# A ring of four work tiles with slots of 4352 bytes, and one head's softmax division moved up 450 places in a planner's list

## The chip, the cores and the metric

The kernel runs on one core of a Trainium2 chip. Its time is the device time of one execution in microseconds (us). Two kernels are compared by the medians of several executions each. The profile is of one execution and gives each engine's instructions: PE is the matrix engine, PEld its weight loads, DVE the vector engine, ACT the scalar engine, POOL the GpSimd engine, and SP the queue that issues most of the DMAs.

## The reference

The program is one layer of a decoder trunk over 1040 positions (16 meta tokens and 1024 tokens) and 1024 channels, in float32:

```python
h = rms_norm(h_res, pre_norm_g[i])
z = h @ w_in[i]                       # 1024 x 7328
y_a = (pool_mixer(...)      * silu(pg)) @ w_out_pool[i]
y_b = (mla_attention(...)   * silu(mg)) @ w_out_mla[i]     # 8 heads
y_c = (conformer_conv(...)  * silu(cg)) @ w_out_conf[i]
y_d = (short_conv(...)      * silu(sg)) @ w_out_sc[i]
m = gts[0] * y_a + gts[1] * y_b + gts[2] * y_c + gts[3] * y_d
h_res = h_res + rms_norm(m @ w_o[i], post_norm_g[i])
```

In the attention a head's scores are masked causally, put through a softmax and multiplied with the values. The division by the softmax's sum is done last, on the head's 64 x 1024 output: that is the "division" of this document.

## The kernel before, in words

Each float32 operand of a matrix product is split in a high and a low part, and a product is made as three products of the parts (`split`, line 498: ACT copies the high part, POOL or DVE subtracts it to get the low part). The two big projections use a Strassen scheme, so their operands are sums of blocks. Work goes in three stages.

**Stage one** (to line 1405) makes `z` by the input projection. PE goes through the blocks of `w_in`; beside it, four lanes of small tasks run (lines 1353 to 1363): convolutions, the attention's queries, keys and values, norms, the splitting of weights. Their tiles come from rings of slots. One of them is the ring `t4` (line 566), four slots in pool `tp`, which hold tiles of up to 4160 bytes a partition: parts of `x`, `cq`, `qn`, `ckv`, `khl`, `vhl` and others, and `kone` (line 983), a row of -1.0 that goes to DRAM once.

**Stage two** (lines 1410 to 1702) is the attention, in 16 steps of one head `h` and one half `c` of the queries. Between the products of a head, `refill` (line 1644) puts in the output projections of the three other branches (`fills`, line 1603). One such unit is six products into a bank `ps_y`, of which there are two, an evacuation `th <- (th + 1) * ps_y` on DVE and an addition `m <- m + th`, most of them on DVE. The next but one unit can begin only when the evacuation has emptied its bank.

For heads 0 to 6 the division is done by `sums` (line 1558) and `head_out` (line 1584): a DMA takes the row of sums out of `ol` into `lc`, DVE takes its reciprocal, a DMA writes it to DRAM (`r`), a DMA reads it back broadcast over 64 partitions (`rb`), and DVE multiplies the halves of `ol` with it into `op[c]`. For the last head PE itself spreads the reciprocals (`sums_pe`, line 1569). Heads come in pairs: after the second head of a pair, POOL multiplies `op[c]` with the gate (`smg`), and `split` makes `boM[c][h // 2]` of it, ACT the high part and POOL the low part. Each of `rb`, `op[0]` and `op[1]` has one slot.

**Stage three** (from line 1707) is the attention's own output projection into `ps_u`, which needs all `boM`, and then the last projection `w_o` with the final norm.

**What sets the order.** Nothing is issued when it is recorded. `Plan.record` gives each operation a number `prio = len(self.ops) - self.lift` (line 336), and `plan.ahead(n)` adds n to `lift` for what is recorded inside it: a positive n moves an operation up, a negative one down. `Plan.flush` (line 364) then plays the recorded stage through with rough costs of its own and, whenever an engine is free, gives it the ready operation of the smallest number whose slots are free (line 418). The order that comes out is what each engine runs, in that order and without overtaking. A DMA counts in it as landed 4500 ns after its transfer (line 448), and in `sums` 5000 ns more for those into SBUF (line 1562). Each stage ends with a `flush`, so no operation of a stage can go behind one of the next. Fills are recorded with -400 (line 1648), the division of heads 0 to 6 with -450, and the last head's with 300 (line 1691).

**Where the tiles lie.** `Pool.lay_out` (line 186) rounds a slot up to the pool's grain, 64 bytes for `tp` and `up`, and 256 bytes for the large pools, whose start it also moves to 64 bytes past a multiple of 256 (`PLACE`). Pools of stages two and three begin again where `const` ends, so their places do not depend on `tp`.

## Time and profile before

| | |
|---|---|
| median of 3 runs | 969.21 us (969.03 to 969.52) |
| the profiled execution | 968.91 us |
| its span, first to last instruction | 967.1 us |
| busy: PE, DVE, POOL, ACT | 950.4, 696.0, 678.0, 449.1 us |
| mean granted clock of PE | 0.997 |

A row of the timeline has the start, the duration, the engine, the line, the operation, what is written and read, and the shape; `x2` are two instructions in one row, and square brackets hold the time that the engine was idle before it, with what ended it. All instructions are recorded through one helper and so have line 362; they are told apart by their tiles.

### The profile page before, as it was taken

What the parts mean: (1) busy time and instruction counts of PE and PEld (TensorE: products, weight loads), DVE (VectorE), ACT (ScalarE), POOL (GpSimd) and SP (SyncE); (2) the same over time, 40 slices, a digit from 0 to 9 for tenths busy, and PEclk for the clock granted to TensorE, in tenths of its full rate; (3) what the DMA queues carried; (4) which work ended last, traced back from release to release, by engine and by line L of the source; (5) the groups of instructions that cost most, each with busy time, mean ns of one, the idle gap of its engine ahead of it and who ended that gap; (6) DMA issues with size and microseconds to landing.
All of it is one profiled execution on the core that took longest, in us unless ns stands there. A gap on an engine that the chain in (4) does not pass through costs nothing.

```text
span 967.1 us, 15247 instructions
## 1 busy us (share of the span) xinstructions
PE 950.4 (98%) x5003; PEld 808.9 (84%) x5003; DVE 696.0 (72%) x1113; ACT 449.1 (46%) x914; POOL 678.0 (70%) x628
## 2 busy tenths in 40 slices
PE   8999999999999999999999999999999999999996
PEld 7999899889888887888888878888888788788885
DVE  5856959988779855544536768346778889799757
ACT  7743233444344455554444344366555555225622
POOL 5957555666576787896679679655567786647955
PEclk9999999999999999999999999999999999999998
DMA  8145566668787687787655688699899664783633
GB/s 258 45 126 144 167 198 213 216 196 270 231 265 255 205 248 214 220 255 216 195 168 169 205 268 276 208 318 262 272 221 297 175 187 132 272 267 95 211 113 142
DMA packets 136330, 203.03 MB, mean 210 GB/s; under 512 B 19672, under 2 KB 83159, under 8 KB 135483
## 3 DMA queue, kind: packets, MB, share of 16 engines
q1 hardware_dynamic: 127274, 185.28, 63.3%
q10 hardware_dynamic: 8656, 15.74, 4.4%
q0 software_dynamic: 320, 1.05, 0.3%
q8 instruction: 39, 0.64, 0.3%
q14 instruction: 41, 0.33, 0.1%
HBM read 129.11 MB, written 72.88 MB: 209 GB/s over the span
## 4 chain that ended last, share of the span: by engine, by line
PE 90%; POOL 3%; DVE 2%; issue 2%; ACT 1%; DMA 1%; DVEq 0%; SPq 0%; POOLq 0%; ACTq 0%
PE ps_pa L362 16%; PE ps_pb L362 16%; PE ps_pc L362 15%; PE ps_o L362 9%; PE ps_y L362 8%; PE ps_s L362 8%; PE ps_pd L362 7%; PE ps_u L362 7%; PE ps_x L362 5%; POOL S L362 1%; POOL lsq L362 1%; ACT junk L362 1%; DVE c L362 0%; DMA lacc<-acc 0%; POOL u L362 0%
## 5 line engine op out<-in xcount | busy, mean ns | idle before, releaser
L362 PE MATMUL ps_pb<-T,S 128*128 128x512 f32 (+2 forms) x792 | 172.0, 359 | 0.0
L362 PE MATMUL ps_pa<-B,A 128*128 128x512 f32 (+2 forms) x792 | 171.7, 360 | 0.0
L362 POOL TENSOR_TENSOR A<-raw,A 128x512 fp32r<-128x512 f32 x84 | 114.3, 1368 | 61.3 <-ACT A L362 47.7
L362 PEld LDWEIGHTS ps_pb<-T,S 128*128 128x128 f32 x792 | 134.3, 189 | 22.4 <-issue 1.2
L362 PEld LDWEIGHTS ps_pa<-B,A 128*128 128x128 f32 x792 | 134.4, 188 | 22.3 <-issue 1.0
L362 POOL TENSOR_TENSOR S<-ss,S 128x512 fp32r<-128x512 f32 x84 | 116.0, 1393 | 51.8 <-ACT S L362 51.7
L362 POOL TENSOR_TENSOR pt<-p,pt 128x512 fp32r<-128x512 f32 (+1 forms) x96 | 102.8, 1094 | 52.5 <-PE ps_s L362 32.6
L362 DVE TENSOR_TENSOR u<-ps_pb,u 128x512 f32<-128x512 f32 (+2 forms) x66 | 40.3, 610 | 87.4 <-PE ps_pb L362 84.3
L362 DVE SCALAR_TENSOR_TENSOR ps_w<-conv,par,ps_w 128x512 f32<-128x512 f32 x116 | 87.1, 751 | 2.3
L362 PE MATMUL ps_y<-bo,whl 128*128 128x512 f32 x288 | 85.7, 403 | 0.9 <-DVE th L362 0.9
L362 PE MATMUL ps_pc<-B,S 128*128 128x512 f32 (+1 forms) x396 | 85.8, 358 | 0.0
L362 ACT ACTIVATE S<-ss 128x512 fp32r<-128x512 f32 x84 | 50.4, 627 | 74.5 <-DVE ss L362 43.7
L362 PE MATMUL ps_pd<-T,A 128*128 128x512 f32 (+2 forms) x396 | 84.9, 359 | 0.0
L362 PE MATMUL ps_pc<-T,S 128*128 128x512 f32 (+1 forms) x396 | 84.4, 359 | 0.0
L362 ACT ACTIVATE p<-ps_s 128x512 f32<-128x512 f32 (+4 forms) x112 | 49.7, 444 | 60.3 <-PE ps_s L362 29.2
L362 PEld LDWEIGHTS ps_pc<-T,S 128*128 128x128 f32 x396 | 66.8, 188 | 11.2 <-issue 0.7
L362 PEld LDWEIGHTS ps_pd<-T,A 128*128 128x128 f32 x396 | 67.1, 189 | 10.7
L362 PEld LDWEIGHTS ps_pc<-B,S 128*128 128x128 f32 x396 | 66.4, 189 | 10.2
L362 PE MATMUL ps_o<-pt,vt 128*128 128x512 f32 (+7 forms) x288 | 68.7, 346 | 0.2 <-ACT ol L362 0.2
L362 PE MATMUL ps_s<-qt,kt 100*128 100x512 f32 (+4 forms) x336 | 67.8, 324 | 0.0
L362 PEld LDWEIGHTS ps_s<-qt,kt 100*128 100x128 f32 (+1 forms) x336 | 54.1, 176 | 10.3 <-DVE qt L362 0.6
L362 ACT ACTIVATE A<-raw 128x512 fp32r<-128x512 f32 x84 | 52.0, 626 | 22.3 <-PE ps_pd L362 9.7
(281 smaller groups left out, 1890.4 us busy)
## 6 DMA issues: line engine op xcount, KB each, us to landing
raw<-in_w_in_dram SPq DMA_DIRECT2D x52, 512.0 KB
th<-th SPq DMA_DIRECT2D x32, 512.0 KB
th<-z ACTq DMA_DIRECT2D x60, 256.0 KB
v<-vhl SPq DMA_DIRECT2D x16, 384.0 KB
qt<-q SPq DMA_DIRECT2D x16, 384.0 KB
vt<-v SPq DMA_DIRECT2D x8, 768.0 KB
bo<-bo SPq DMA_DIRECT2D x6, 1024.0 KB
w_out_mla<-whl SPq DMA_DIRECT2D x16, 256.0 KB
```

The source lines that it names most:

```text
L362: getattr(self.handle[o["eng"]], o["op"])(*map(real, o["args"]), **{k: real(v) for k, v in o["kw"].items()})
```

## The change

The tile `kone` is made with 1088 columns, of which the first 1040 are used as before, so the largest tile of the ring `t4` has 4352 bytes and each of its four slots gets as many. The division of head 6, the seventh of the eight, is recorded with 0 and not with -450: its three DMAs (`lc`, `r`, `rb`), its reciprocal and its two multiplications stand 450 places further up in the list. Nothing is computed otherwise, and no instruction is added or taken away.

```diff
@@ -980,7 +980,7 @@
-        t = t4([4, L], name="kone")
+        t = t4([4, LK], name="kone")[:, :L]
         POOL.memset(t, -1.0)
         ld(ones_dram, t)
@@ -1688,7 +1688,7 @@
-        with plan.ahead(300 if h == H - 1 else -450):
+        with plan.ahead(300 if h == H - 1 else 0 if h == H - 2 else -450):
             if h == H - 1:
                 head_out(h, c, sums_pe(h, c))
             elif c:
```

`L` is 1040 and `LK` is 1088 (lines 35 and 50); the block of line 1691 does something only for `c == 1` where `h` is 0 to 6.

## The prediction, made before the changed kernel was built

> **What bounds the kernel now.** I read the page's busy times first, then the busy times by stage, then PE's waits, then the timeline where a wait falls behind the change.

> ```profile
> PE 950.4 (98%) x5003; PEld 808.9 (84%) x5003; DVE 696.0 (72%) x1113; ACT 449.1 (46%) x914; POOL 678.0 (70%) x628
> ```
> ```profile
> 25.00:300.00 275.00, 274.37 (x1750) 249.62 (x1750) 220.82 (x347) 114.99 (x243) 179.72 (x167) 1.00 0.61 190
> 300.00:640.00 340.00, 339.22 (x1510) 277.81 (x1509) 198.95 (x262) 152.15 (x277) 261.58 (x235) 1.00 0.73 223
> ...
> 826.00:838.00 12.00, 11.09 (x54) 8.40 (x53) 11.54 (x18) 1.86 (x3) 6.45 (x6) 1.00 0.67 242
> 838.00:958.00 120.00, 119.96 (x541) 99.55 (x539) 98.05 (x118) 47.96 (x96) 81.26 (x59) 1.00 0.53 178
> 958.00:967.00 9.00, 0.00 (x0) 0.00 (x0) 5.45 (x12) 0.90 (x4) 3.79 (x4) 0.64 0.47 176
> ```
> ```profile
> PE ps_s L362 <- ACT p L362: 1.0, 1, 1.0
> PE ps_y L362 <- DVE th L362: 0.9, 1, 0.9
> ```

> PE's column follows the length of each stretch: 274.4 of 275, 339.2 of 340, 120.0 of 120. So PE is the bound, at a clock of 1.00, and time goes only where PE idles: 0.9 us in 826 to 838, and the last 9 us, which have no product at all. Of PE's waits the second row is the one in reach of the change: the unit of fills that waits for an evacuation `th`. That bounds what the change can give directly.

> ```profile
> 833.16 2.34 PE L362 MATMUL ps_y<-bo,whl 128*128 128x512 f32 x9
> 836.41 1.67 PE L362 MATMUL ps_y<-bo,whl 128*128 128x512 f32 x6 [0.91 <-DVE th L362]
> ```
> ```profile
> 825.41 0.69 DVE L362 SCALAR_TENSOR_TENSOR th<-th,ps_y 128x512 f32<-128x512 f32 x1 [3.58 <-PE ps_y L362]
> 826.13 0.84 DVE L362 TENSOR_TENSOR m<-m,th 128x512 f32<-128x512 f32 x1
> 827.00 0.68 DVE L362 TENSOR_TENSOR op<-ol,ps_s 64x512 f32<-64x512 f32 x1
> 827.72 0.69 DVE L362 SCALAR_TENSOR_TENSOR th<-th,ps_y 128x512 f32<-128x512 f32 x1
> 828.44 0.69 DVE L362 TENSOR_TENSOR m<-m,th 128x512 f32<-128x512 f32 x1
> ...
> 829.76 1.07 DVE L362 TENSOR_TENSOR m<-m,th 128x512 f32<-128x512 f32 x1
> ...
> 831.46 0.69 DVE L362 TENSOR_TENSOR m<-m,th 128x512 f32<-128x512 f32 x1
> 832.31 0.69 DVE L362 SCALAR_TENSOR_TENSOR th<-th,ps_y 128x512 f32<-128x512 f32 x1 [0.16 <-PE ps_y L362]
> ...
> 834.47 1.29 DVE L362 TENSOR_TENSOR op<-ol,rb 64x512 f32<-64x512 f32 x2
> 835.68 0.67 DVE L362 SCALAR_TENSOR_TENSOR th<-th,ps_y 128x512 f32<-128x512 f32 x1
> ```

> The last eight units of fills run here. DVE starts on their evacuations at 825.41, after 3.58 us of idling, and from there has one gap, of 0.16 us. The two multiplications of head 6 at 834.47 (1.29 us for both) stand directly ahead of the sixth evacuation, at 835.68. The eighth unit needs the bank of the sixth, so PE begins it at 836.41 and not 0.91 us earlier. DVE is the local bound of these ten microseconds, and PE pays only for what DVE has not done in time.

> **Part one, the ring.** The slots of `t4` are 4160 bytes, 64 more than a multiple of 256, so by `lay_out` they start 64, 128, 192 and 0 bytes past such a multiple; with 4352, which is 17 x 256, all start at 64. What follows in stage one moves by 768 bytes, 3 x 256, and keeps that remainder. The later pools stay. Stage one's list knows slots by number and not by place, so its order stays too. What is left is the speed of reads and writes at another place. Successive tiles lie in different slots, so rows of one kind tell:

> ```profile
> 332.45 0.60 ACT L362 ACTIVATE qn<-ps_x 128x512 fp32r<-128x512 f32 x1 [5.86 <-PE ps_x L362]
> 337.99 0.60 ACT L362 ACTIVATE qn<-ps_x 128x512 fp32r<-128x512 f32 x1 [0.41 <-PE ps_x L362]
> ```

> They are equal to 0.01 us. From below, PE's 274.4 of 275 and 339.2 of 340 leave 1.4 us of idling that faster tiles could remove in these two stretches. From above, if each of some 100 (an estimate) ACT, DVE and POOL instructions on the ring grew by 0.01 us, that would be 1 us in 600, beside a PE that waits for none of them. I take 0. If PE's cover were gone, the 1 us would count. Two slots of stage two (`pt`) come to lie over another neighbour of stage one; both sides' use ends before the first `pt`, so I take 0 there too.

> **Part two, the division.** It moves seven things: three DMAs on SP's queue, the reciprocal, the two multiplications. First the reciprocal.

> ```profile
> 813.80 1.67 DVE L362 TENSOR_TENSOR op<-ol,rb 64x512 f32<-64x512 f32 x1
> ...
> 817.69 0.34 DVE L362 RECIPROCAL lc<-lc 32x32 f32<-32x32 f32 x1
> ...
> 818.61 1.50 DVE L362 TENSOR_TENSOR m<-m,th 128x512 f32<-128x512 f32 x1
> ```
> ```profile
> 802.53 0.54 SPq L362 DMA_DIRECT2D lc<-ol  x1
> ```
> ```profile
> 813.80 0.32 SPq L362 DMA_DIRECT2D th<-th  x1
> 818.06 0.32 SPq L362 DMA_DIRECT2D r<-lc  x1
> ...
> 821.86 0.32 SPq L362 DMA_DIRECT2D th<-th  x1
> 822.27 0.46 SPq L362 DMA_DIRECT2D rb<-r  x1
> ```

> The DMA of `lc` is issued at 802.53, at once, and does not move. The reciprocal runs at 817.69, behind the two masks' work and head 5's multiplications. In front of these it would run near 812.5 to 813.5. Its 0.34 us then delays DVE for some 5 us, and is given back before the idle 3.58 us that end at 825.41: 0. `r` moves past one `th` in SP's queue and waits for the reciprocal there; that `th` is issued at 813.80, so it loses at most 0.3 us, and its evacuation is 10 us away. `rb` needs `r` (4.2 us from 818.06 to 822.27, a wait for a `th` in it) and the slot that head 5's second multiplication, at 815.78, frees: it goes out at about 817.3, ahead of a `whl` at 818.47. So `rb` comes some 5 us earlier, 822.27 less 817.3. No row holds its landing, but head 1's bounds it:

> ```profile
> 705.28 0.46 SPq L362 DMA_DIRECT2D rb<-r  x1
> ```
> ```profile
> 712.24 1.29 DVE L362 TENSOR_TENSOR op<-ol,rb 64x512 f32<-64x512 f32 x2
> ```

> It was there 7.0 us after its issue at the latest, and so head 6's is by about 824.3.

> Then the multiplications. They can't use the 3.58 us: `op[0]` is one slot, still read by POOL's `boM` until 826.42, and `op[1]` until 830.27:

> ```profile
> 825.12 1.30 POOL L362 TENSOR_TENSOR boM<-op,boM 128x512 fp32r<-128x512 f32 x1
> 826.38 1.74 POOL L362 TENSOR_TENSOR op<-op,smg 128x512 f32<-128x512 f32 x1
> ...
> 828.93 1.34 POOL L362 TENSOR_TENSOR boM<-op,boM 128x512 fp32r<-128x512 f32 x1 [0.51 <-ACT boM L362]
> 835.23 3.36 POOL L362 TENSOR_TENSOR op<-op,smg 128x512 f32<-128x512 f32 x2 [4.96 <-DVE op L362]
> 838.55 3.44 POOL L362 TENSOR_TENSOR boM<-op,boM 128x512 fp32r<-128x512 f32 x2
> ```

> So the first goes behind the second evacuation, near 828.4 (the planner counts 4.5 + 5.0 us for `rb`, which puts it there), and the second near 832. Both stay inside DVE's busy stretch and ahead of the sixth evacuation. DVE's work up to that point is therefore the same, and the wait of 0.91 us is not removed but spread: with 0.68 us more ahead of the third evacuation and again ahead of the fourth, the fifth and sixth units each start later, and the eighth still waits for the sixth evacuation.

> What changes is POOL. Its 4.96 us of idling, a wait for these multiplications, end early, and its four operations of 1.7 us move from 835.23 to 842, where PE does not wait for DVE, into DVE's stretch. An addition takes 0.69 us alone (828.44, 831.46) and 1.07 beside a POOL operation (829.76, beside the one at 828.93). By my order: addition 2, pushed beside POOL's operation of 828.93, +0.38; addition 3, beside one now as then, 0; the second multiplication, at the end of one, +0.1; addition 4, beside the second gate multiplication, +0.38; addition 5, 0. The sum is 0.38 + 0.1 + 0.38 = **+0.9 us**: the sixth evacuation ends and the eighth unit begins 0.9 us later. After 838 PE is full and `boM` is there earlier than before, so the shift stays as it is until the end.

> From both sides: below, all of the 0.91 us goes and no addition collides, -0.9. Above, additions 2, 4 and 5 cost 1.50 each (818.61, beside POOL's gate multiplication) and both multiplications the middle of this row, 1.39 and not 0.65:

> ```profile
> L362 DVE TENSOR_TENSOR op<-ol,rb x14: 677/1388/1779, 688.7 to 835.1; 64x512 f32<-64x512 f32 x14
> ```

> That is 3 x 0.81 + 2 x 0.74 = +3.9. I take the 1.07 of the nearest row, 829.76, the same addition in the same stretch.

> [...]

> **The sum**: 968.91 profiled, which is 0.30 under the median; the median is what is compared, so 969.21 + 0.9 = **970.1 us**, 0.09% more. A measurement of this kernel tells about 0.2%, 1.94 us, from no change: between 967.3 and 971.1 counts as the same.

> **The rivals.**
> - *The wait goes.* The multiplications fit without delaying an evacuation: 969.2 - 0.9 = 968.3. For it: the division's 5 us of lead. Against: DVE's single gap of 0.16 us in the stretch, and the slots of `op`.
> - *Nothing happens.* The list puts the division where it was, since slots and not numbers decide it: 969.2. Against: the reciprocal ran behind work that doesn't need the slots.
> - *POOL shuts DVE out* (slower). The upper prices hold: 969.2 + 3.9 = 973.1. It decides once collisions add more than 1.94 us, five additions at 1.07 or three at 1.50. For it: 1.67 and 1.50 in the rows of 813.80 and 818.61. Against: 829.76.
> - *Another list to the end* (faster). From the division on, the planner plays through other times, and the last nine microseconds, all DVE and POOL, can come out in another order. Rows of that end:

> ```profile
> 960.18 1.20 DVE L362 SCALAR_TENSOR_TENSOR u<-u,rso,xr 128x512 f32<-128x512 f32 x1 [0.19 <-POOL rso L362]
> 961.31 0.74 DVE L362 SCALAR_TENSOR_TENSOR c<-c,rso,xr 128x512 f32<-128x512 f32 x1
> ```

> One such collision gone is 0.46; with two of them gone, the wait of 0.91 and the collisions of additions 1 and 3 (0.15 + 0.38) it is 969.2 - 2.4 = 966.8. For it: PE-less end. Against: stage three follows PE, which does not change its pace.

> **How the numbers follow.** Forecast 0.37, the wait goes 0.13, nothing 0.08: together 0.58 within 0.2%. POOL shuts DVE out 0.27, slower. Another list 0.15, faster. Cases of both signs are in it; the forecast's own range, half a collision more or less per addition, is 969.2 to 971.1. The whole range goes from the fast rival to just under the slow one, 966.9 to 973.0, which leaves out half of either, 0.07 + 0.13.

> **What would show it.** Right: up to 810 us every PE row at its old time; the reciprocal before head 5's multiplications; `op<-ol,rb` near 828 and 832; POOL without its 4.96 us; several short waits of PE for `th` in place of one, 0.9 us longer in sum; the stage after 838 shifted whole. Wrong: a PE total in stage one that moved by over 0.5 us (the ring has a price), or a PE wait after 840 (the list has changed further on than I followed it).

## The result and the profile after

The changed kernel took **978.11 us** (median of 6 executions, 974.13 to 982.22), the kernel before 969.22 us beside it: a ratio of 1.0090 (95% interval 1.0076 to 1.0104). It is slower, and its executions lie 8 us apart where those of the kernel before lie 0.6 us apart. The profiled execution took 977.9 us, with a span of 975.7 us, 8.6 more than before.

The busy times of the page and the busy times by stage, of the changed kernel (the columns of a stretch are its length, then busy time and count of PE, PEld, DVE, ACT and POOL, then PE's granted clock, DMA share and GB/s):

```profile
PE 954.8 (98%) x5003; PEld 812.7 (83%) x5003; DVE 694.4 (71%) x1113; ACT 448.9 (46%) x914; POOL 677.3 (69%) x628
```
```profile
25.00:300.00 275.00, 274.37 (x1750) 249.64 (x1749) 222.10 (x348) 115.04 (x243) 179.77 (x167) 1.00 0.62 190
300.00:640.00 340.00, 339.26 (x1515) 278.27 (x1514) 198.81 (x264) 152.80 (x278) 262.42 (x236) 1.00 0.73 224
826.00:838.00 12.00, 11.98 (x61) 9.23 (x59) 7.58 (x12) 5.25 (x13) 11.41 (x11) 1.00 0.31 106
```
```profile
640.00:690.00 50.00, 49.39 (x271) 41.56 (x271) 32.87 (x92) 33.18 (x79) 30.70 (x40) 1.00 1.01 291
690.00:697.70 7.70, 3.50 (x22) 2.73 (x21) 3.83 (x9) 3.69 (x8) 3.45 (x3) 0.95 1.04 234
697.70:703.70 6.00, 6.00 (x15) 4.73 (x16) 2.75 (x6) 0.05 (x1) 0.00 (x0) 0.50 1.06 228
703.70:766.00 62.30, 61.77 (x337) 52.17 (x336) 46.71 (x110) 35.89 (x86) 43.74 (x46) 1.00 0.77 226
```

Stage one is what it was: 274.37 and 339.26 against 274.37 and 339.22. The loss is in stage two, 120 us ahead of the division. For 4.2 us of 690 to 697.7 PE does nothing, and in the six microseconds after that its clock is 0.50, so that by my estimate from the clock 6.0 us of products do the work of 3.0 (the first ten of them took 4.10 us, 697.70 to 701.80; the same ten took 2.24 us, 694.64 to 696.88, in the profile of E13, at a clock of 1.00). PE's busy time is 4.4 us higher in total though it does the same products, and these 3.0 are in it: slow work counts as busy. Together that is 4.2 + 3.0 = 7.2 of the 8.6 us; two further short gaps, 0.61 in the first row and 0.53 in the last, bring it to 8.3. (The stretch from 826 to 838 holds other work than before, since everything has moved by some 8 us.)

PE's waits of the changed kernel, and then the chain of work that ended last, in order of time:

```profile
PE ps_s L362 <- DMA qt<-q: 4.2, 1, 4.2
```
```profile
682.40 1.03 PE ps_y L362 x5
683.43 14.13 DMA qt<-q
697.57 0.14 issue
697.70 0.61 PE ps_s L362
```

A load of the queries (`qt` of head 3, second half) is issued at 683.43 and lands 14.1 us later; PE wants it at 693.5. The timeline of PE says why it wants it then. First the changed kernel, then the one before:

```profile
692.94 0.22 PE L362 MATMUL ps_s<-qt,kt 100*16 100x16 f32 x3
693.02 0.47 PE L362 MATMUL ps_y<-bo,whl 128*128 128x512 f32 x1
697.70 0.61 PE L362 MATMUL ps_s<-kt,qt 96*128 96x328 f32 x1 [4.20 <-DMA qt<-q]
698.11 1.91 PE L362 MATMUL ps_y<-bo,whl 128*128 128x512 f32 x4
...
701.80 4.05 PE L362 MATMUL ps_o<-pt,vt 128*128 128x512 f32 x13
```
```profile
692.08 0.94 PE L362 MATMUL ps_y<-bo,whl 128*128 128x512 f32 x3
692.85 3.16 PE L362 MATMUL ps_o<-pt,vt 128*128 128x512 f32 x13
695.85 0.27 PE L362 MATMUL ps_s<-ident,mr 128*4 128x128 f32 x1
695.88 0.55 PE L362 MATMUL ps_s<-kt,qt 96*128 96x328 f32 x2
```

Before, thirteen products of 3.16 us stood ahead of the first use of this `qt`; in the new list they stand behind it. So PE asks for it 2.4 us earlier. The load did not move with it (SP issued it at 683.87 before). By the trace it landed at 695.05 in the kernel before, 0.8 us ahead of its use. The old list had no more to spare than that.

How the list came to change is in the planner. Played through, its list of stage one is the same in all 5388 operations, and in stage two 1885 of 1972 have other planned times with the ring's edit alone, 134 with the division's alone (all from the division on). The ring's part comes through two places in the code: `lay_out` gives each slot of a new stage the time at which the last tile of the old stage lying over the same bytes is done with, and `flush` makes an event of each such time. The planner looks for something to issue only when an event comes up.

```python
sl["after"] = max((last for p, last in self.past if ...
                   and p[1] < y and x < p[2]), default=0)
...
for sl in g["slots"]:
    if sl["after"]:
        heapq.heappush(events, (sl["after"], 1, 0))
```

With everything behind the ring moved up 768 bytes, one slot of `pt` no longer lies over stage one's `u3` but only over `z`, and its time goes from 639.8 to 632.8 us on the planner's clock. No `pt` is put in it before 646 us, so the slot itself changes nothing. The event does: at 632.8 the planner finds that a load waiting on SP may go, which it had seen only at the next event, at 633.5. That load is 0.64 us earlier in the plan, and each later choice of the smallest ready number sees other times. An event put in at 632.8 us by hand, with the ring and all slot times as before, gives the order of the wider ring whole (14 planned times differ); at 58 other times, every 1.7 us from 622 to 719, it gives the plan before, but for the times of two operations once.

### The profile page after: what moved, and what is told of

Read it like the earlier page. It is cut to its first block, busy times and chain, and to the rows that moved or that the text cites. A ratio compares the mean times of both kernels' runs of the same rounds, so it can differ in the third digit from the quotient of the medians.

```text
span 975.7 us, 15238 instructions
## 1 busy us (share of the span) xinstructions
PE 954.8 (98%) x5003; PEld 812.7 (83%) x5003; DVE 694.4 (71%) x1113; ACT 448.9 (46%) x914; POOL 677.3 (69%) x628
## 4 chain that ended last, share of the span: by engine, by line
PE 86%; DMA 4%; POOL 3%; DVE 3%; issue 2%; ACT 1%; SPq 0%; DVEq 0%; POOLq 0%; ACTq 0%
PE ps_pa L362 16%; PE ps_pb L362 15%; PE ps_pc L362 14%; PE ps_o L362 9%; PE ps_u L362 7%; PE ps_pd L362 7%; PE ps_s L362 7%; PE ps_y L362 7%; PE ps_x L362 4%; DMA qt<-q 2%; POOL S L362 1%; DMA vs<-v 1%; DMA x<-in_x_dram 1%; POOL lsq L362 1%; DVE op L362 1%
## 5 line engine op out<-in xcount | busy, mean ns | idle before, releaser
L362 PE MATMUL ps_pb<-T,S 128*128 128x512 f32 (+2 forms) x792 | 171.8, 359 | 0.0
L362 PE MATMUL ps_pa<-B,A 128*128 128x512 f32 (+2 forms) x792 | 171.6, 360 | 0.0
L362 POOL TENSOR_TENSOR A<-raw,A 128x512 fp32r<-128x512 f32 x84 | 114.4, 1369 | 60.2 <-ACT A L362 50.2
L362 POOL TENSOR_TENSOR S<-ss,S 128x512 fp32r<-128x512 f32 x84 | 116.1, 1395 | 53.1 <-ACT S L362 53.1
L362 PEld LDWEIGHTS ps_pb<-T,S 128*128 128x128 f32 x792 | 134.4, 189 | 22.2 <-issue 1.2
L362 PEld LDWEIGHTS ps_pa<-B,A 128*128 128x128 f32 x792 | 134.3, 188 | 22.2 <-issue 1.0
L362 POOL TENSOR_TENSOR pt<-p,pt 128x512 fp32r<-128x512 f32 (+1 forms) x96 | 102.7, 1095 | 60.6 <-PE ps_s L362 31.7
L362 DVE TENSOR_TENSOR u<-ps_pb,u 128x512 f32<-128x512 f32 (+2 forms) x66 | 40.3, 611 | 86.9 <-PE ps_pb L362 83.8
L362 DVE SCALAR_TENSOR_TENSOR ps_w<-conv,par,ps_w 128x512 f32<-128x512 f32 x116 | 87.2, 752 | 2.3
L362 PE MATMUL ps_y<-bo,whl 128*128 128x512 f32 x288 | 87.0, 410 | 1.2 <-DVE th L362 1.1
L362 PE MATMUL ps_pc<-B,S 128*128 128x512 f32 (+1 forms) x396 | 85.8, 358 | 0.0
L362 ACT ACTIVATE S<-ss 128x512 fp32r<-128x512 f32 x84 | 50.5, 627 | 76.0 <-DVE ss L362 47.7
L362 PE MATMUL ps_pd<-T,A 128*128 128x512 f32 (+2 forms) x396 | 84.9, 359 | 0.0
L362 PE MATMUL ps_pc<-T,S 128*128 128x512 f32 (+1 forms) x396 | 84.4, 359 | 0.0
L362 ACT ACTIVATE p<-ps_s 128x512 f32<-128x512 f32 (+4 forms) x112 | 49.7, 444 | 62.9 <-PE ps_s L362 30.2
L362 PEld LDWEIGHTS ps_pc<-T,S 128*128 128x128 f32 x396 | 66.8, 189 | 11.3 <-issue 0.7
L362 PEld LDWEIGHTS ps_pd<-T,A 128*128 128x128 f32 x396 | 67.1, 189 | 10.7
L362 PEld LDWEIGHTS ps_pc<-B,S 128*128 128x128 f32 x396 | 66.4, 189 | 10.1
L362 PE MATMUL ps_o<-pt,vt 128*128 128x512 f32 (+7 forms) x288 | 69.3, 351 | 0.7 <-ACT ol L362 0.7
L362 PE MATMUL ps_s<-qt,kt 100*128 100x512 f32 (+4 forms) x336 | 67.8, 324 | 0.5 <-ACT p L362 0.5
L362 ACT ACTIVATE A<-raw 128x512 fp32r<-128x512 f32 x84 | 52.0, 626 | 22.0 <-PE ps_pd L362 9.6
L362 PEld LDWEIGHTS ps_s<-qt,kt 100*128 100x128 f32 (+1 forms) x336 | 54.1, 177 | 9.6 <-ACT p L362 0.7
```

What stands on the lines that cost most here:

```text
L362: getattr(self.handle[o["eng"]], o["op"])(*map(real, o["args"]), **{k: real(v) for k, v in o["kw"].items()})
```

## The experiments

The theory before them, "list": the ring's edit reorders stage two, and that makes the whole loss. Its rivals: "places" (tiles at other addresses are slower) and "division". After E1 to E4 the theory became "margin": the new list costs a little always, and leaves one load so little time that PE waits for it in some executions. Its rival was "both": the two parts together do what neither does alone.

All times are medians in us, with lowest and highest and the number of executions; the ratio is to the kernel before on the same chip, with its 95% interval. The ratio is the record's estimate and lies nearer to the quotient of the means than to that of the medians, so single high executions weigh in it. E1 to E4 ran on one chip, E5 to E8 on a second, E9 to E12 on a third, E13 and E14 on the second again.

| | what | us | ratio |
|---|---|---|---|
| E1 | ring alone | 970.54 (969.54 to 972.42, 11) | 1.0011 (1.0003 to 1.0020) |
| E2 | division alone | 969.73 (969.12 to 970.83, 11) | 1.0001 (0.9992 to 1.0010) |
| E3 | new places, old list | 968.66 (967.69 to 970.11, 11) | 0.9993 (0.9984 to 1.0001) |
| E4 | old places, new list | 971.82 (970.03 to 981.48, 12) | 1.0030 (1.0013 to 1.0048) |
| E5 | the change again | 971.54 (971.17 to 975.13, 8) | 1.0027 (1.0017 to 1.0037) |
| E6 | ring alone again | 971.15 (969.77 to 976.73, 11) | 1.0023 (1.0008 to 1.0038) |
| E7 | both parts, old list | 969.42 (968.81 to 970.23, 11) | 1.0000 (0.9991 to 1.0009) |
| E8 | the change, qt 6 places earlier | 971.38 (970.98 to 971.71, 11) | 1.0018 (1.0009 to 1.0027) |
| E9 | the change, qt 2 places later | 977.47 (976.32 to 979.12, 4) | 1.0081 (1.0068 to 1.0094) |
| E10 | before, qt 2 places later | 971.53 (969.63 to 975.87, 11) | 1.0027 (1.0016 to 1.0039) |
| E11 | before, qt 3 places later | 975.73 (975.19 to 976.26, 5) | 1.0061 (1.0048 to 1.0074) |
| E12 | E11 with PE kept busy | 974.73 (973.25 to 975.03, 5) | 1.0046 (1.0034 to 1.0058) |
| E13 | the change, third measurement | 971.36 (970.39 to 979.00, 12) | 1.0024 (1.0008 to 1.0039) |
| E14 | E8 beside E13 | 971.41 (970.84 to 973.23, 11) | 1.0018 (1.0009 to 1.0026) |

**E1 and E2, one part each.** Each is one of the two hunks of the change.

> Only the first part of the change: the ring's slots are 4352 bytes, the division stays where it was. Theory 'list': the wider ring lets the planner count one of stage two's slots for pt as free 7.0 us earlier, that moves the list of stage two, and in it the load of qt comes too late for PE (4.2 us of idle) and the clock is granted at 0.5 for some 7 us after it. That happens near 697 us, 120 us ahead of the division, so it is all here: 977 us (974 to 982), with a PE wait on qt of 3 to 5 us and a stretch of half clock near 697 us. Rival 'places' (tiles at other addresses are slower to read or write): also 977, but without need of the PE wait. Rival 'division': 969.2 (968.8 to 969.6), no such wait.

> Only the second part of the change: the seventh head's division 450 operations later in rank, the ring as before. Theory 'list' and rival 'places' both: nothing of the 8.9 us is here; the list is the same up to the division, so no PE wait of over 1 us between 640 and 766 us. What is left is the prediction's own second part, 970.1 (968.3 to 973.1): reciprocals near 812 us rather than 817, multiplications near 814 and 816, the 5 us idle of POOL ahead of its op ended earlier. Rival 'division': 978, with PE waiting between 810 and 845 us.

The division alone is the kernel before within a tenth of a per cent, so the rival "division" falls. (Its multiplications ran at 828.46 and 831.44, not at the 814 and 816 of this expectation; the prediction had put them at 828.4 and 832.) But the ring alone is only 0.11% slower, not 0.8%, although its list is that of the changed kernel up to the division. The size in theory "list" falls too: the new list alone doesn't make 978.

**E3 and E4, places and list apart.** In `lay_out`, E3 takes the ring's edit and holds the old slot times; E4 has the ring as before and takes the new ones:

```diff
 E3:  -  and p[1] < y and x < p[2]), default=0)
      +  and p[1] < y + 768 and x < p[2]), default=0)
 E4:  +  and p[1] < y - 768 and x < p[2]), default=0)
```

> The wider ring, with the planner made to see stage two's slots as free no earlier than before, so that the list of all three stages is the list before, instruction for instruction; only the addresses differ from the kernel before. Theory 'list': 969.2 (968.8 to 969.7). Rival 'places': 977.

> The ring as before (4160 bytes), with the planner made to see the slot for pt as free at the earlier time, so that the list is that of the wider ring alone, instruction for instruction, on the old addresses. Theory 'list': 977 (974 to 982), with the PE wait on qt and the half clock near 697 us. Rival 'places': 969.2 (968.8 to 969.7).

New places with the old list cost nothing: the rival "places" falls. The new list on the old places is slower by 2.2 us in the median, and has what the first measurement had: one execution of 981.48, which weighs in its ratio too. Its median is far below the 977 expected. So the new list does two things: a steady loss of one to two microseconds, and now and then a large one.

**E5 to E8: is it the two parts together, or the margin of one load?** E7 is the change with E3's edit. In E8 one transfer is moved in SP's queue after the planner is done, six places up (`early` is set on the load of `qt[3, 1]` alone):

```diff
+        for o in [o for o in order if o.get("early")]:
+            sp = [x for x in order if x["eng"] == "SP"]
+            order.remove(o)
+            order.insert(order.index(sp[sp.index(o) - o["early"]]), o)
         for o in order:
             self.issue(o)
```

> The changed kernel itself, unaltered, beside the next three on one chip. Up to 822 us its list and its addresses are those of the ring alone, which took 970.54 us (969.54 to 972.42). Theory 'margin' (the new list has PE reach the load of qt with nothing to spare, and how long PE then waits, 0 to some 5 us, with or without the half clock behind it, depends on how fast the transfers are in that execution and on that chip): as the ring alone on this chip, 970 to 974, with some executions at 977 and more. Rival 'both' (the two parts together do something that neither does alone): 976 to 980 here too, while the ring alone stays at 970.5.

> The ring alone once more, beside the changed kernel on the same chip. Theory 'margin': within 0.2% of the changed kernel's median, whatever that is on this chip. Rival 'both': 970.5, some 7.5 us below the changed kernel.

> Both parts of the change, but the planner sees stage two's slots as free no earlier than before, so the list is that of the division alone, instruction for instruction. Theories 'list' and 'margin': 969.3 (968.5 to 970), as the places under the old list (968.66) and the division alone (969.73) were. Rival 'both': 976 to 980.

> The changed kernel with one transfer moved: the load of the qt that PE waited 4.2 us for is issued six places earlier on SP, ahead of two loads of bo, one of whl, the rb, one of th and the write of lc (3.3 MB ahead of it less); every engine's list is otherwise unaltered. Theory 'margin': no wait of PE on that qt and no half clock at 697 us, 969.8 to 971 on any chip, and no execution above 974; the bo loads land 1 to 2 us later, which nothing waits for if they had that to spare. Rival 'list' in general (the loss is spread over the new order, the wait on qt only shows it): as the changed kernel beside it, with the wait moved to another row.

The change and the ring alone are alike here (971.54 and 971.15), each with executions of 975 and more; with the old list both parts together cost nothing. That is theory "margin", and the rival "both" falls. In the profile of E5 the same products meet the same load, 2.6 us less late (timeline of PE):

```profile
693.84 0.47 PE L362 MATMUL ps_y<-bo,whl 128*128 128x512 f32 x1
695.94 0.39 PE L362 MATMUL ps_s<-kt,qt 96*128 96x328 f32 x1 [1.63 <-DMA qt<-q]
```

With the load ahead of those transfers (3.1 MB by their sizes, not the 3.3 of the expectation) the wait is gone in E8 and so are the high executions: all eleven lie within 0.73 us. The median, 971.38, is hardly below E5's and lies above the 971 that was expected. What is left between 640 and 766 us are these waits of PE in E8; below them the same stretch of the kernel before, where PE idles for 0.02 us:

```profile
PE ps_o L362 <- ACT ol L362: 0.5, 1, 0.5
PE ps_s L362 <- ACT p L362: 0.5, 1, 0.5
```
```profile
640.00:766.00 126.00, 125.98 (x682) 105.54 (x682) 95.22 (x236) 77.05 (x179) 81.88 (x90) 1.00 0.92 264
```

These are the same two gaps as in the changed kernel's stretches, 1.0 us of the 1.55 by which E8 is slower than the kernel before. So the rival "spread over the new order" is right for these 1.0 us; where the other half microsecond is lost stays open. For the large loss it is wrong.

**E9 to E12: the wait by the dose, and the clock.** E9 to E11 move the same load the other way; E12 puts 24 products that need no `qt` ahead of the waiting one.

```diff
+            after = sp[sp.index(o) + o["late_by"]]
+            order.remove(o)
+            order.insert(order.index(after) + 1, o)
 E12:
+            if getattr(self, "fill", None) in o.get("bufs", ()) and o["eng"] == "PE":
+                s, _, k = (v.real() for v in o["args"][:3])
+                for _ in range(24):
+                    self.handle["PE"].matmul(s, k[:, :128], k, start=True, stop=True)
+                self.fill = None
```

> The changed kernel with the load of that one qt issued two places later on SP (behind one load of whl and one of th, 0.75 MB); every engine's list is otherwise unaltered. Theory 'margin': the load lands 2 to 3 us later, PE waits 4 to 5 us for it in nearly every execution and the clock goes to 0.5 behind the wait: 976 to 980, the 978.11 of the first measurement, on a chip where the changed kernel itself takes 971.5. Rival (the first measurement's loss had another source): 973 to 974.5, the 2 to 3 us of later landing alone, without the half clock.

> The kernel before, its list and its addresses, with the load of the same qt issued two places later on SP (behind one load of whl and one of th). Theory 'margin': in the kernel before the load landed at 695.05 us and PE took it at 695.88, so it has 0.8 us to spare; landing where th landed (697.6 to 698.6) it makes PE wait 1.8 to 2.7 us, too short for the half clock: 971.4 to 972.6. Rival: the old list has more to spare than that, 969.6.

> The kernel before with the load of the same qt issued three places later on SP (behind whl, th and kt, 1.06 MB). Theory 'margin': it lands where kt landed (near 700.4 us), PE waits 4 to 5 us and the clock goes to 0.5 for 3.4 or 6.8 us: 969.6 + 4.5 + 1.7 or 3.4 = 975.8 to 977.5, in a kernel that has nothing of the change. Rival (the half clock isn't PE's idle time, but belongs to the new list): 974, without a stretch of half clock.

> As the one before (three places later), with 24 matmuls of 328 columns added on PE ahead of the first that needs the qt; what they write is overwritten by it. They take 24 x 0.146 = 3.5 us, within the wait. If the half clock follows from PE standing idle: the wait is filled, the clock stays at 1.0, 973.5 to 975, that is 1.7 to 3.4 us less than without them although PE does more work. If the half clock follows from the transfers or the stall itself: as without them, or longer.

E9 gives the first measurement's time, with the same wait, 4.16 us, and a half clock behind it. (The changed kernel as it is was not run on that chip, so the 971.5 of the expectation is another chip's.) E10 has the expected median, but more spread than expected: the profiled execution, at 975.87, waited 3.6 us and had the half clock that I had thought out of reach. That 1.8 to 2.7 us are too short for it was my estimate, and not shown: a wait of 1.88 us in E11 was followed by it (last section). E11 is E9 in a kernel without any of the change: a wait of 3.5 us, below the 4 to 5 expected, the half clock behind it, and a median at the lower end of what was expected. Its profile has a second stretch of half clock at 9.36 us; that one belongs to the start of this execution and not to the load, so not all of the 7.2 us by which its span is longer are the load's. The waiting row of E11 in PE's timeline, and its stretches:

```profile
701.18 0.57 PE L362 MATMUL ps_s<-kt,qt 96*128 96x328 f32 x2 [3.53 <-DMA qt<-q]
```
```profile
702.00:706.00 4.00, 4.00 (x17) 3.53 (x17) 1.53 (x4) 0.10 (x1) 0.00 (x0) 0.57 0.58 106
706.00:710.00 4.00, 4.00 (x22) 3.57 (x21) 2.68 (x8) 2.66 (x5) 1.75 (x2) 1.00 0.49 143
```

And of E12, where L475 is the line of the added products:

```profile
696.32 3.85 PE L475 MATMUL ps_s<-kt 96*128 96x328 f32 x24
700.01 0.46 PE L362 MATMUL ps_s<-kt,qt 96*128 96x328 f32 x2
```
```profile
696.00:700.00 4.00, 4.00 (x27) 3.82 (x27) 0.68 (x1) 1.31 (x6) 2.73 (x5) 1.00 1.04 293
700.00:704.00 4.00, 4.00 (x26) 3.60 (x25) 2.17 (x5) 0.60 (x1) 0.00 (x0) 1.00 0.15 38
```

In the four microseconds behind the wait the granted clock is 0.57 in E11 and 1.00 in E12, and 17 products run against 26. The load is as late in E12: it landed at 699.76, 3.4 us after the added products began. So in this pair the half clock follows from PE standing idle, not from the late load. All five executions of E11 have a mean clock of 0.994 or 0.995, all five of E12 0.996 or 0.997. In time the 24 products save 1.0 us, less than the 1.7 to 3.4 expected, and the two intervals overlap. They took 3.85 us, not the 3.5 of the expectation; they end at 700.17, 0.4 us past the landing, and so use up a little of what they save.

**E13 and E14: once more.**

> The changed kernel once more, in another measurement. Theory 'margin': a median anywhere from 971 to 979, with executions over 974 showing a lower mean clock (0.992 to 0.996) than those at 971 (0.997 to 0.998). Rival (the first measurement was of something that has passed): 971.5 with a spread of 1 us.

> The changed kernel with the load of that qt six places earlier on SP, beside the one above. Theory 'margin': 971.4 (970.9 to 972), no wait on qt, whatever the changed kernel itself takes here. Rival: it moves with the changed kernel.

E13's median is 971.36, with single executions of 974.01 and 979.00 at mean clocks of 0.995 and 0.993, the others at 0.996 to 0.998. In E14 the highest is 973.23, and one execution of the kernel before reached 973.01 in that measurement. The two medians are alike, so they decide nothing, and E13's expectation was so wide that it could hardly fail; what differs are the high executions. Above 974 us lie 3 of 20 of the change (E5, E13) and none of 22 with the load moved up (E8, E14). At a rate of 3 in 20, 22 without one come about once in 35 times by chance. (E14's profile has a wait of 0.9 us ahead of 695.60, for rows of a `qt` that DVE writes and not for this load.) PE in the profile of E13:

```profile
693.71 0.47 PE L362 MATMUL ps_y<-bo,whl 128*128 128x512 f32 x1
694.64 0.39 PE L362 MATMUL ps_s<-kt,qt 96*128 96x328 f32 x1 [0.47 <-ACT p L362]
```

The same list, and a wait of 0.47 and not 4.20 us. The view puts it down to ACT, but the load's last part landed at 694.51, and the row begins 0.135 us later. In all seven profiles of this list in which the load was not moved up (the first, E1, E4, E5, E6, E9, E13) that row begins 0.135 us after the landing, be it at 693.97 (E6) or at 697.57 (the first). So PE takes up this load the moment it is there, and there is nothing to spare in any of them; with the old list (the kernel before, E2, E3, E7) it lands 0.8 to 1.2 us ahead of its use. What differs between the first profile and E13 are the transfers. The queue that holds nearly all of them, from 670 to 700 us (packets, MB, share of 16 engines' time), in the changed kernel's first profile, in E13 and in the kernel before:

```profile
q1 hardware_dynamic: 2499, 7.71, 98.7%
```
```profile
q1 hardware_dynamic: 2479, 7.73, 90.3%
```
```profile
q1 hardware_dynamic: 2429, 7.64, 87.0%
```

In the execution that waited 4.2 us, the same 7.7 MB took 98.7 and not 90.3% of the transfer engines' time, 9% more. That is one execution of each.

## Why the prediction was wrong

**What failed** is one sentence of part one: "Two slots of stage two (`pt`) come to lie over another neighbour of stage one; both sides' use ends before the first `pt`, so I take 0 there too." I asked whether the slot is late for its tile, and it isn't. I did not ask who else reads its time. That time is also an event in `flush`, and through it the ring's edit gives nearly all of stage two other planned times and changes the order on every engine. It holds for the steady loss (E4 against E3: the list on the old places is slower, the new places under the old list are not) and for the large one (E8, E9).

**"Up to 810 us every PE row at its old time"** failed with it. PE waits at 693.5, ahead of anything that I had followed. My list of rivals had "another list to the end", but only from the division on and only as a gain. The later medians of the same program, 971.54 (E5) and 971.36 (E13), lie inside my range of 966.9 to 973.0, but that is luck: their 1.7 to 1.8 us are there with the ring's list and gone with the old one (E7), and my sum had nothing for it.

**That PE is full was read as cover.** PE's 126.0 of 126 us of work between 640 and 766 says that it waits for nothing. It doesn't say by how little. The load of `qt` landed 0.8 us ahead of its use, in a stretch where the transfers take 87% to 99% of the engines' time. I looked at no load's landing in stage two outside the division.

**Part one, the places**, was right: E3 is at 0.9993 (0.9984 to 1.0001), and stage one's stretches did not move.

**Part two** was right in its order, by the profile of E2, and only in part in its sum. DVE, SP and PE of E2:

```profile
812.28 0.33 DVE L362 RECIPROCAL lc<-lc 32x32 f32<-32x32 f32 x1
...
825.73 1.38 DVE L362 TENSOR_TENSOR m<-m,th 128x512 f32<-128x512 f32 x1
...
828.46 0.68 DVE L362 TENSOR_TENSOR op<-ol,rb 64x512 f32<-64x512 f32 x1
829.06 0.68 DVE L362 TENSOR_TENSOR m<-m,th 128x512 f32<-128x512 f32 x1
...
830.37 1.06 DVE L362 TENSOR_TENSOR m<-m,th 128x512 f32<-128x512 f32 x1
...
831.44 0.65 DVE L362 TENSOR_TENSOR op<-ol,rb 64x512 f32<-64x512 f32 x1
...
832.73 1.06 DVE L362 TENSOR_TENSOR m<-m,th 128x512 f32<-128x512 f32 x1
...
835.25 1.22 DVE L362 TENSOR_TENSOR m<-m,th 128x512 f32<-128x512 f32 x1
836.39 0.68 DVE L362 SCALAR_TENSOR_TENSOR th<-th,ps_y 128x512 f32<-128x512 f32 x1
```
```profile
817.32 0.47 SPq L362 DMA_DIRECT2D rb<-r  x1
```
```profile
835.27 1.66 PE L362 MATMUL ps_y<-bo,whl 128*128 128x512 f32 x6 [0.86 <-DVE th L362]
837.12 1.65 PE L362 MATMUL ps_y<-bo,whl 128*128 128x512 f32 x6 [0.18 <-DVE th L362]
```

The reciprocal comes at 812.28 (I had 812.5 to 813.5), `rb` at 817.32 (817.3), the multiplications at 828.46 and 831.44 (828.4 and 832). The eighth unit begins at 837.12 and not 836.41, 0.71 us later, where the sum had 0.9. That this is so near is partly luck. Of the three terms only addition 4 came as I had it (1.06 us); addition 2 (0.68) and the second multiplication (0.65) met no collision, while additions 1 and 5, which the sum had at nothing, took 1.38 and 1.22 us where the kernel before has 0.84 and 0.69, and DVE began the stretch 0.41 us earlier. The medians can't tell: 1.0001 (0.9992 to 1.0010) leaves anything from -0.8 to +1.0 us.

**What stays open.** In the first measurement all six executions were above 974 us; later, with the same program, one of 8 (E5) and two of 12 (E13). That the wait depends on what goes ahead of the load in the queue is shown (E8, E9). That slower transfers made the first measurement's wait rests on the two rows of the queue. What makes them slower in some executions, and why in all six of the first measurement, is not known; on which chip that measurement ran is not on record. Of the executions above 974 us in E4, E5, E6 and E13 none was profiled. That they are the same wait is argued from their mean clocks, 0.992 to 0.996, and not seen.

## What to carry to other kernels

When an order comes out of a planner that plays the work through, a change of a place or a slot is a change of the list, and the list is compared as a whole before its effect is argued away, above all where the planner's events come from more than the operations. When PE is full, look for the load with the least time between landing and use, not only for waits: a list that uses it 2.4 us earlier turned 0.8 us to spare into a wait of 0 to 4 us. In E11 such a wait of 3.5 us cost half as much again through the clock, by my estimate: 1.7 us, half of the 3.413 us at half clock. The remedy for the large loss is to give that one load its place in the queue; the steady 1.5 us stay (E8, E14).

## What the runs showed of the hardware that I had not expected

The length of a wait alone did not decide. Waits of 3.53 (E11), 3.59 (E10), 4.16 (E9) and 4.20 us (the changed kernel) were followed by half clock; 1.63 us (E5), 2.24 us (the kernel before) and 2.42 us (E3), the last two at the start of the run, were not. But 1.88 us, at the start of E11, was: PE in its timeline, and a stretch around the half clock that the records have from 9.36 to 12.77 us.

```profile
9.15 0.97 PE L362 MATMUL ps_x<-ident,x 128*128 128x128 f32 x4 [1.88 <-DVE x L362]
```
```profile
9.30:12.80 3.50, 3.50 (x18) 3.50 (x18) 2.86 (x5) 2.66 (x7) 1.03 (x3) 0.51 1.09 363
```

That wait, from 7.27 to 9.15, lies whole in one step of the grid (5.94 to 9.36), while the 2.24 and the 2.42 us lie across a boundary: in the kernel before, from 6.69 to 8.93, 1.47 us in one step and 0.77 in the next, which begins at 8.16. Laid on the grid, the sixteen traces agree without an exception: PE idled 1.88 us or more in each of the 21 steps of full clock that half clock followed (16 of them where the products end), and at most 1.83 us in each that full clock followed. In the changed kernel PE idled through the whole step ahead of the half clock at 696.91 (693.50 to 696.91); the step ahead of E11's half clock at 702.26 was not idle as a whole, it held 2.33 us of idling and 1.08 us of products.

One of the sixteen parts of a load was much later than the others. Of the `qt` in the changed kernel's profile fifteen parts had landed by 695.78 and the last at 697.57; in E13 by 692.19 and at 694.51. So 1.8 of the 4.2 us that PE waited were for one part of sixteen.
